# All merge gates computed ahead of the branch projections, 20 of 24 tiles by the Strassen scheme, and kept in DRAM

## The chip, the cores and the metric

The kernel runs on one core of one Trainium2 chip. The metric is the device time of one execution, in microseconds (us). The kernel before took 2695.42 us, the median of three runs (2694.82 to 2695.98).

The engines are named as in the profile: PE is TensorE (matmuls; its weight loads are PEld), DVE is VectorE, ACT is ScalarE, POOL is GpSimd and SP is SyncE, whose queue issues nearly all of the transfers. Each engine works through its own list of instructions in order.

## The reference, cut to what matters

One layer of a hybrid decoder block on 1024 tokens and 16 meta tokens, with a model width of 1024. Three branches (gated DeltaNet, Mamba-2 SSD, sliding-window attention) each give a 1024-wide output. Each is projected, weighted by a sigmoid gate per channel and token, and the three are added:

```python
u = rmsnorm(h, norm1_w[l]) @ w_in[l]
(..., gate_logits) = split_in(u)
gates = jax.nn.sigmoid(gate_logits)
g_a, g_b, g_c = jnp.split(gates, N_BRANCH, axis=-1)
merged = (g_a * (y_gdn @ w_proj_gdn[l]) + g_b * (y_ssd @ w_proj_ssd[l])
          + g_c * (y_swa @ w_proj_swa[l]))
h = h + merged @ w_out[l]
hn = rmsnorm(h, norm2_w[l])
h = h + jnp.square(jax.nn.relu(hn @ w_up[l])) @ w_down[l]
```

The gate logits are a product of the normed input (1024 x 1024 tokens) with 3 x 1024 columns of the input weights. The sigmoid is worked out as half of (1 + tanh of half the logit).

## The kernel before, in words

Activations lie transposed: 128 channels on the partitions, tokens along the row, in halves of 512 tokens. A matrix of 1024 channels is eight such tiles k by two halves c. Every fp32 operand is split into a high and a low part (ACT copies it to the rounded high part, DVE or POOL subtracts that from the original), and every product is three matmuls: high by high, high by low, low by high.

The normed input is kept all along as tiles hnh (high) and hnl (low). A gate tile is 128 of the 3 x 1024 gate channels of branch b, called (b, m) with m from 0 to 7: merge_gates loads and splits its weights (split_w: load to mgr, ACT copy mgh, POOL subtraction mgl) and runs for each half 24 matmuls into a bank mgm (gemm, L148); ACT's tanh (L1047) leaves the gate in a tile gt, of which there are four buffers. A projection tile (b, m) is merge_proj: weights wpr, split to wph and wpl, then 48 matmuls into two banks pr (L1063), and DVE operations that weight them with the gate and add them up in mg (L1070, L1073, L1074).

stage_merge walks the 24 tiles, all of branch 0 first. In each step it issues the gate tile two steps ahead and then the projection tile, so that PE goes from one to the other: 48 matmuls mgm, 48 matmuls pr, and so on. The first two gate tiles, and the weights of the third (w2), are issued during the attention branch. At the first tile of a branch, merge_load reads the branch's output back from DRAM: 16 halves, each loaded into one of four buffers yr (the ring "r"), copied to yh by ACT (L135) and subtracted to yl by DVE (L136). The 32 tiles yh and yl of one branch are one set of buffers, so that the next branch's take their place.

The order on each engine is set by a scheduler that places the instructions by its own estimate of when operands and buffers come free; the program's text is only its starting point. After the merge come stage_out (output projection, bank pso, L1115) and the MLP, whose up projection (bank up, L1209) is already done by the Strassen scheme, with the mixed activations prepared by u_mix.

Of the kernel before, what the change touches and what calls it, by code (L numbers as in the profile page):

```python
# [7 lines left out]
F32 = mybir.dt.float32  # L8
F32R = mybir.dt.float32r
U32 = mybir.dt.uint32  # L10
AF = mybir.ActivationFunctionType
ALU = mybir.AluOpType
# [4 lines left out]
P = 128  # L17
D = 1024
KT = D // P
SEQ = 1024  # L20
META = 16
# [27 lines left out]
W_M = 68  # L49
# [2 lines left out]
KW = SEQ + 4 * META  # L52
NM = 17
NPR = NFF // 2
HOIST = 2
WL, WR, WY, WS = 1800, 3200, 2000, 2200

# [5 lines left out]
class Trunk:  # L63
    def __init__(self, ctx, tc, I, out):
# [32 lines left out]
        self.gad = self.dram.tile([3 * KT, P, SEQ], F32, name="gad")  # L97
        self.acd = self.dram.tile([NPR, 7, P, 512], F32, name="acd")
        self.hd = self.dram.tile([NB, P, D], F32, name="hd")
# [939 lines left out]
    def gate_w(self, b, m):  # L1039
        return self.split_w(self.I["win"][W_M + KT * b + m], "mg")  # L1040

    def merge_gates(self, b, ms, w=None):
        nc = self.nc
        for m in ms:
            for c0, n, ps in self.gemm(w or self.gate_w(b, m), (self.hnh, self.hnl), CH_REAL, "mgm"):
                t = self.tp.tile([P, 512], F32, name="gt", tag="t", bufs=4)
                nc.scalar.activation(t, ps, AF.Tanh, scale=0.5)  # L1047
                self.gates[m, (c0 - META) // 512] = t

    def merge_load(self, b):  # L1050
        place = lambda n: self.half("y", 4 * KT, n)
        self.y = [[self.split_half(self.yd[b][k][:, 512 * c:512 * c + 512], "y", place, self.nc.vector)
                   for c in range(2)] for k in range(KT)]

    def merge_proj(self, b, m):
        nc = self.nc
# [19 lines left out]
    def stage_merge(self, w2):  # L1076
        self.mg = {}
        seq = [(b, m) for b in range(3) for m in range(KT)]
        for i, (b, m) in enumerate(seq):
            if m == 0:  # L1080
                self.merge_load(b)
            if i < len(seq) - 2:
                self.merge_gates(seq[i + 2][0], (seq[i + 2][1],), w2 if i == 0 else None)
            self.merge_proj(b, m)


    def stage_out(self):
# [63 lines left out]
    def split(self, src, hi, lo, eng=None):  # L1151
        nc = self.nc
        nc.scalar.activation(hi, src, AF.Copy)  # L1153
        (eng or nc.vector).tensor_tensor(lo, src, hi.bitcast(F32), op=ALU.subtract)  # L1154
        return hi, lo
# [154 lines left out]
    def stage_up(self):  # L1310
        self.u_prep(1)
        pre = [self.up_hoist(0)]
        for k in range(4):
            self.u_tile(1, k)
            self.u_tile(1, k + 4)
        pre += [self.up_hoist(j) for j in range(1, HOIST)]
        self.u_mix()
        for j in range(NPR):
            self.up_pair(j, pre[j] if j < HOIST else None)

    def stage_down(self):
# [12 lines left out]
        for p0, n in ((0, 6), (6, 5), (11, 5)):  # L1334
            first, lastc = p0 == 0, p0 + n == NPR
            prs = range(p0, p0 + n)
# [132 lines left out]
def build(ctx, tc, I, out):  # L1469
    k = Trunk(ctx, tc, I, out)  # L1470
    nc = tc.nc
    pool = lambda st, name, **kw: st.enter_context(tc.tile_pool(name=name, **{"bufs": 1, **kw}))
    ph, ps, px = ExitStack(), ExitStack(), ExitStack()
    k.px = ExitStack()
    k.pa = ExitStack()
    with nc.allow_non_contiguous_dma(reason="layout"):
        k.tp = pool(ctx, "tp")
        k.hn = pool(ph, "hn", side="right")
        k.c2 = pool(k.pa, "c2")
        k.sp = pool(ps, "smp", side="right")  # L1480
        k.xp = pool(px, "xp", side="right", bufs=3)
        k.stage_norm()
        px.close()
        k.open_branches()
        cur = k.gdn_first()
        k.stage_small()
        ps.close()
        k.open_gdn()
        k.stage_gdn(cur)
        k.open_rest()  # L1490
        k.stage_ssd()
        k.open_psum()
        store = k.stage_swa()
        k.gates = {}
        k.merge_gates(0, (0, 1))
        w2 = k.gate_w(0, 2)
        store()
        k.px.close()
        k.pa.close()
        k.pbx.close()  # L1500
        k.pdr = pool(ctx, "pdr", space=PSUM, reuse_waits="tile")
        k.lp = pool(ctx, "lp", reuse_waits="tile")
        k.stage_merge(w2)
        ph.close()
        k.rp = pool(ctx, "rp", side="right", reuse_waits="tile")
        k.stage_out()
        k.stage_mlp()
    return k
# [73 lines left out]
```

## Time and profile before

| what | value |
|---|---|
| median of three runs | 2695.42 us |
| the profiled execution | 2700.42 us |
| its span | 2698.7 us |
| PE busy | 2547.8 us (94%) |
| DVE, ACT, POOL busy | 1608.3, 1034.7, 614.7 us |
| stage that the change touches | 1419 to 1932 us of the span |
| HBM read, written | 179.56 MB, 52.70 MB |

A row of the chain of waits gives start, length and what it was: an engine's run of instructions, or a transfer that was waited for. The chain runs back from the end, so what stands in it set the end at that place. A row of the timeline gives start, length, engine, line, operation, the tiles written and read, sizes, how many, and in brackets the idle time of the engine before it and what ended it. A row of the windows gives busy time and count of each engine in a stretch, then the granted PE clock as a share, the DMA share and GB/s. Matmul ends are modelled, and a few records can be missing.

### The profile page before, as it was taken

How to read it: one execution, taken by the hardware profiler on the slowest of the kernel's cores; microseconds unless marked ns; L12 is line 12 of the kernel's file. 1: busy time of each engine (PE TensorE's matmuls, PEld its weight loads, DVE VectorE, ACT ScalarE, POOL GpSimd, SP SyncE). 2: the span in 40 equal slices, each digit the busy share in tenths (PEclk: the TensorE clock that was granted, in tenths of full speed). 3: DMA queues.
4: the chain of work that ended last, by engine and by line, in shares of the span. 5: the costliest groups of instructions: out<-in, count | busy, mean ns of one | idle time of the engine just before them, and what ended most of it. 6: DMA issues, size and time to landing. Idle time of an engine off the chain costs nothing.

```text
span 2698.7 us, 37432 instructions
## 1 busy us (share of the span) xinstructions
PE 2547.8 (94%) x13983; PEld 2178.5 (81%) x13983; DVE 1608.3 (60%) x3039; ACT 1034.7 (38%) x2581; POOL 614.7 (23%) x479
## 2 busy tenths in 40 slices
PE   6999999999999999999999999999998999989997
PEld 5887888887888988888887888878876888768886
DVE  5776767767466766577762022232428777586887
ACT  4434444434332332355552121121345444344443
POOL 3322222222133232321211222222340000040230
PEclk8989999999899999999999999999998999989999
DMA  3211211111111121321213131131323434655422
GB/s 117 70 37 53 61 53 53 53 36 60 47 55 63 63 79 63 95 56 52 60 48 125 47 110 47 47 109 48 129 100 127 164 149 152 241 191 192 143 92 86
DMA packets 120916, 241.14 MB, mean 89 GB/s; under 512 B 39478, under 2 KB 39894, under 8 KB 120734
## 3 DMA queue, kind: packets, MB, share of 16 engines
q1 hardware_dynamic: 116526, 230.98, 25.6%
q0 software_dynamic: 3200, 6.43, 1.2%
q8 instruction: 110, 1.80, 0.3%
q10 hardware_dynamic: 1008, 1.34, 0.2%
q14 instruction: 72, 0.59, 0.1%
HBM read 179.56 MB, written 52.70 MB: 86 GB/s over the span
## 4 chain that ended last, share of the span: by engine, by line
PE 75%; DVE 16%; issue 3%; DMA 2%; ACT 2%; POOL 1%; ACTq 0%; SPq 0%; DVEq 0%; POOLq 0%
PE dn L1365 11%; PE up L1209 11%; PE mgm L148 9%; PE pr L1063 9%; PE pso L1115 3%; PE aq L148 3%; PE x L148 3%; PE gg L148 2%; PE v L148 2%; PE q L148 2%; DVE xt L512 2%; PE z L148 2%; PE b L148 2%; PE c L148 2%; PE k L148 1%
## 5 line engine op out<-in xcount | busy, mean ns | idle before, releaser
L1154 POOL TENSOR_TENSOR wl<-wd,wh 128x512 fp32r<-128x512 f32 x48 | 71.6, 1497 | 521.7 <-DMA ar<-acd 340.1
L1365 PE MATMUL dn<-wh,ah 128*128 128x512 f32 x448 | 175.5, 393 | 14.5 <-ACT wh L1153 14.5
L1365 PE MATMUL dn<-wl,ah 128*128 128x512 f32 x448 | 176.2, 394 | 6.0 <-DVE wl L1154 5.4
L1365 PE MATMUL dn<-wh,al 128*128 128x512 f32 x448 | 175.6, 392 | 0.0
L1063 PE MATMUL pr<-yh,wph 128*128 128x512 f32 x384 | 150.0, 391 | 2.9 <-ACT yh L135 1.8
L1063 PE MATMUL pr<-yl,wph 128*128 128x512 f32 x384 | 150.1, 391 | 1.7 <-DVE yl L136 1.7
L1063 PE MATMUL pr<-yh,wpl 128*128 128x512 f32 x384 | 149.5, 389 | 0.0
L1073 DVE SCALAR_TENSOR_TENSOR gt<-gt,pr 128x512 f32<-128x512 f32 x32 | 21.9, 687 | 201.8 <-PE pr L1063 201.8
L1154 DVE TENSOR_TENSOR al<-ar,ah 128x512 fp32r<-128x512 f32 x112 | 98.7, 884 | 51.3 <-ACT ah L1153 51.1
L1153 ACT ACTIVATE ah<-ar 128x512 fp32r<-128x512 f32 x112 | 70.2, 627 | 125.0 <-PE dn L1365 90.5
L124 POOL TENSOR_TENSOR wpl<-wpr,wph 128x1024 fp32r<-128x1024 f32 x24 | 61.1, 2547 | 231.0 <-ACT wph L122 220.4
L1365 PEld LDWEIGHTS dn<-wh,ah 128*128 128x128 f32 x448 | 85.1, 190 | 32.9 <-ACT wh L1153 15.0
L122 ACT ACTIVATE wph<-wpr 128x1024 fp32r<-128x1024 f32 x24 | 25.5, 1061 | 215.0 <-PE pr L1063 195.6
L1365 PEld LDWEIGHTS dn<-wl,ah 128*128 128x128 f32 x448 | 85.1, 190 | 24.7 <-DVE wl L1154 6.1
L148 PE MATMUL mgm<-hnh,mgh 128*128 128x512 f32 x384 | 100.1, 398 | 2.1 <-ACT gt L1047 2.1
L148 PE MATMUL mgm<-hnl,mgh 128*128 128x512 f32 x384 | 99.9, 399 | 0.0
L148 PE MATMUL mgm<-hnh,mgl 128*128 128x512 f32 x384 | 99.5, 396 | 0.0
L1365 PEld LDWEIGHTS dn<-wh,al 128*128 128x128 f32 x448 | 85.2, 190 | 17.7
L124 POOL TENSOR_TENSOR mgl<-mgr,mgh 128x1024 fp32r<-128x1024 f32 x24 | 57.6, 2398 | 166.1 <-PE mgm L148 157.8
L1063 PEld LDWEIGHTS pr<-yh,wph 128*128 128x128 f32 x384 | 72.1, 188 | 20.2 <-ACT yh L135 3.7
L1063 PEld LDWEIGHTS pr<-yl,wph 128*128 128x128 f32 x384 | 72.1, 188 | 18.8 <-DVE yl L136 3.8
L148 PEld LDWEIGHTS mgm<-hnh,mgh 128*128 128x128 f32 x384 | 72.0, 189 | 18.8 <-ACT gt L1047 2.6
(477 smaller groups left out, 7080.4 us busy)
## 6 DMA issues: line engine op xcount, KB each, us to landing
ar<-acd SPq DMA_DIRECT2D x112, 256.0 KB
wu<-in_wup SPq DMA_DIRECT2D x34, 512.0 KB
acd<-s SPq DMA_DIRECT2D x64, 256.0 KB
mgr<-in_win SPq DMA_DIRECT2D x24, 512.0 KB
wpr<-in_wpr SPq DMA_DIRECT2D x24, 512.0 KB
yr<-yd SPq DMA_DIRECT2D x48, 256.0 KB
acd<-c SPq DMA_DIRECT2D x48, 256.0 KB
dms<-rowd SPq DMA_DIRECT2D x16, 512.0 KB
```

The source lines that it names most:

```text
L122: nc.scalar.activation(wh, wr, AF.Copy)
L124: nc.gpsimd.tensor_tensor(wl, wr, wh.bitcast(F32), op=ALU.subtract)
L148: nc.tensor.matmul(ps[:, 0:n], a[:, k, :], b[k][:, c0:c0 + n], start=(i == 0 and k == 0), stop=(i == 2 and k == KT - 1))
L512: nc.vector.tensor_tensor(tv, lb[:, j:j + 1, j + 1:32].broadcast_to([3 * n_, n, m]), ub[:, 0:n, j:j + 1].broadcast_to([3 * n_, n, m]), op= ...
L1063: nc.tensor.matmul(ps, x[:, k, :], y, start=(k == 0 and j == 0), stop=(k == KT - 1 and j == 2))
L1073: nc.vector.scalar_tensor_tensor(t, t, 1.0, ps, op0=ALU.add, op1=ALU.mult)
L1115: nc.tensor.matmul(ps, x[k, th][:, ts], y, start=(k == 0 and j == 0), stop=(k == KT - 1 and j == 2))
L1153: nc.scalar.activation(hi, src, AF.Copy)
L1154: (eng or nc.vector).tensor_tensor(lo, src, hi.bitcast(F32), op=ALU.subtract)
L1209: self.nc.tensor.matmul(ps, x[:, k * P:(k + 1) * P], ops[k][y], start=(j == 0 and k == 0), stop=(j == 2 and k == 3))
L1365: nc.tensor.matmul(acc[t], x[:, t * P:(t + 1) * P], y, start=(i == 0 and m == 0), stop=(i == n - 1 and m == 2))
```

## The change

All gates are computed before the first projection and go to DRAM. gate_out does the tanh and stores the half to a buffer gad in DRAM; gate_load reads a gate tile back into two of the four gt buffers, two tiles ahead of its use. Tiles 0 to 3 of branch 0 are computed as before. The other 20 form ten pairs of 256 gate channels. For these, the weights and the normed input are each taken as two by two blocks, and the four block products come from seven products of sums and differences (Strassen's scheme in Winograd's form): gp1 to gp7, each 12 matmuls (4 tiles k by 3 split products), together 84 instead of 2 x 48 = 96 for a pair.

gate_mix makes the mixed activations once: it adds hnh and hnl to get the normed input back (hr, in the four buffers of the ring "r"), forms the four sums and differences, and splits them to gh and gl, which lie in the 32 buffers that later take yh and yl. gate_pair makes the mixed and split weights (gah, gal, g1, g2, g3, g4, g22, mostly in the ring "m" of 17 halves), runs the seven products and adds them up to the four results (halves c11, u4, x1 and u2), which also live in ring "r".

After the pairs, the pool of the normed input is closed and a pool yp put in its place for the second branch's yh and yl, so that the outputs of the branches alternate between two sets; the next branch is read from the middle of the one before (m == 4), the first branch after the last pair.

```diff
--- before.py
+++ after.py
@@ -52,6 +52,7 @@
 KW = SEQ + 4 * META
 NM = 17
 NPR = NFF // 2
+NGP = 4
 HOIST = 2
 WL, WR, WY, WS = 1800, 3200, 2000, 2200
 
@@ -1039,18 +1040,136 @@
     def gate_w(self, b, m):
         return self.split_w(self.I["win"][W_M + KT * b + m], "mg")
 
+    def gate_out(self, g, c, ps):
+        t = self.tp.tile([P, 512], F32, name="gt", tag="t", bufs=4)
+        self.nc.scalar.activation(t, ps, AF.Tanh, scale=0.5)
+        self.nc.sync.dma_start(self.gad[g, :, 512 * c:512 * c + 512], t)
+
     def merge_gates(self, b, ms, w=None):
-        nc = self.nc
         for m in ms:
             for c0, n, ps in self.gemm(w or self.gate_w(b, m), (self.hnh, self.hnl), CH_REAL, "mgm"):
-                t = self.tp.tile([P, 512], F32, name="gt", tag="t", bufs=4)
-                nc.scalar.activation(t, ps, AF.Tanh, scale=0.5)
-                self.gates[m, (c0 - META) // 512] = t
+                self.gate_out(KT * b + m, (c0 - META) // 512, ps)
+
+    def gate_load(self, b, m):
+        for c in range(2):
+            t = self.gates[m, c] = self.tp.tile([P, 512], F32, name="gt", tag="t", bufs=4)
+            self.nc.sync.dma_start(t, self.gad[KT * b + m, :, 512 * c:512 * c + 512])
+
+    def gate_mix(self):
+        nc = self.nc
+        tt = nc.vector.tensor_tensor
+        g = self.go = {}
+        y = lambda n: self.half("y", 4 * KT, n)
+        sl = [slice(META + 512 * c, META + 512 * c + 512) for c in range(2)]
+        for k in range(4):
+            r = {}
+            for i in range(2):
+                for c in range(2):
+                    h, l = self.hnh[4 * i + k][:, sl[c]], self.hnl[4 * i + k][:, sl[c]]
+                    if (i, c) != (0, 1):
+                        g[{(0, 0): 0, (1, 0): 1, (1, 1): 2}[i, c], k] = h, l
+                    x = r[i, c] = self.half("r", 4, "hr", F32)
+                    tt(x, h.bitcast(F32), l.bitcast(F32), op=ALU.add)
+
+            def op(p, x):
+                h, l = g[p, k] = y("gh"), y("gl")
+                nc.scalar.activation(h, x, AF.Copy)
+                tt(l, x, h.bitcast(F32), op=ALU.subtract)
+            tt(r[0, 0], r[0, 1], r[0, 0], op=ALU.subtract)
+            op(4, r[0, 0])
+            tt(r[0, 0], r[1, 1], r[0, 0], op=ALU.subtract)
+            op(5, r[0, 0])
+            tt(r[0, 1], r[1, 1], r[0, 1], op=ALU.subtract)
+            op(6, r[0, 1])
+            tt(r[1, 0], r[1, 0], r[0, 0], op=ALU.subtract)
+            op(3, r[1, 0])
+
+    def gate_pair(self, g0, last):
+        nc = self.nc
+        tt = nc.vector.tensor_tensor
+        m = lambda n, dt=F32: self.half("m", NM, n, dt)
+        bank = (lambda n: self.pmm.tile([P, 512], F32, name=n, tag="mm", bufs=3))
+
+        def split(x, n):
+            h, l = m(n + "h", F32R), m(n + "l", F32R)
+            nc.scalar.activation(h, x, AF.Copy)
+            tt(l, x, h.bitcast(F32), op=ALU.subtract)
+            return h, l
+
+        def mm(ps, w, p):
+            for j, (x, y) in enumerate(((0, 0), (0, 1), (1, 0))):
+                for k in range(4):
+                    nc.tensor.matmul(ps, w[x][:, k * P:(k + 1) * P], self.go[p, k][y], start=(j == 0 and k == 0),
+                                     stop=(j == 2 and k == 3))
+        w1 = self.wst.tile([P, D], F32, name="gw1", tag="wr")
+        nc.sync.dma_start(w1, self.I["win"][W_M + g0])
+        w2 = self.wst.tile([P, D], F32, name="gw2", tag="wh")
+        nc.sync.dma_start(w2, self.I["win"][W_M + g0 + 1])
+        a = [w1[:, 0:512], w1[:, 512:D], w2[:, 0:512], w2[:, 512:D]]
+        ah = self.wst.tile([P, D], F32R, name="gah", tag="wl")
+        al = m("gal", F32R), m("gal", F32R)
+        nc.scalar.activation(ah, w1, AF.Copy)
+        for i in range(2):
+            tt(al[i], a[i], ah.bitcast(F32)[:, 512 * i:512 * i + 512], op=ALU.subtract)
+        ps = {}
+
+        def first():
+            ps[0] = self.pd("gp1")
+            mm(ps[0], (ah[:, 0:512], al[0]), 0)
+            x = self.half("r", 4, "x1", F32)
+            nc.scalar.copy(x, ps[0])
+            ps[1] = bank("gp2")
+            mm(ps[1], (ah[:, 512:D], al[1]), 1)
+            c = self.half("r", 4, "c11", F32)
+            tt(c, x, ps[1], op=ALU.add)
+            self.gate_out(g0, 0, c)
+            return x
+
+        def second():
+            s1 = m("gs1")
+            tt(s1, a[2], a[3], op=ALU.add)
+            o1 = split(s1, "g1")
+            tt(s1, s1, a[0], op=ALU.subtract)
+            o2 = split(s1, "g2")
+            s3 = m("gs3")
+            tt(s3, a[0], a[2], op=ALU.subtract)
+            tt(s1, a[1], s1, op=ALU.subtract)
+            ps[5] = self.pc("gp5")
+            mm(ps[5], o1, 4)
+            ps[6] = bank("gp6")
+            mm(ps[6], o2, 5)
+            return s1, s3
+        if last:
+            s4, s3 = second()
+            x1 = first()
+        else:
+            x1 = first()
+            s4, s3 = second()
+        u2 = self.half("r", 4, "u2", F32)
+        tt(u2, x1, ps[6], op=ALU.add)
+        o4 = split(s4, "g4")
+        p3 = self.pc("gp3")
+        o3 = split(s3, "g3")
+        p7 = bank("gp7")
+        for i in ((0, 1) if last else (1, 0)):
+            mm(*(((p7, o3, 6), (p3, o4, 2))[i]))
+        u4 = self.half("r", 4, "u4", F32)
+        tt(u4, u2, ps[5], op=ALU.add)
+        tt(u4, u4, p3, op=ALU.add)
+        self.gate_out(g0, 1, u4)
+        tt(u2, u2, p7, op=ALU.add)
+        o7 = split(a[3], "g22")
+        p4 = self.pc("gp4")
+        mm(p4, o7, 3)
+        tt(x1, u2, ps[5], op=ALU.add)
+        self.gate_out(g0 + 1, 1, x1)
+        tt(u2, u2, p4, op=ALU.add)
+        self.gate_out(g0 + 1, 0, u2)
 
     def merge_load(self, b):
-        place = lambda n: self.half("y", 4 * KT, n)
-        self.y = [[self.split_half(self.yd[b][k][:, 512 * c:512 * c + 512], "y", place, self.nc.vector)
-                   for c in range(2)] for k in range(KT)]
+        place = lambda n: self.half("y", 4 * KT, n, pool=self.yp if b == 1 else self.lp)
+        return [[self.split_half(self.yd[b][k][:, 512 * c:512 * c + 512], "y", place, self.nc.vector)
+                 for c in range(2)] for k in range(KT)]
 
     def merge_proj(self, b, m):
         nc = self.nc
@@ -1076,12 +1195,24 @@
     def stage_merge(self, w2):
         self.mg = {}
         seq = [(b, m) for b in range(3) for m in range(KT)]
+        self.gate_mix()
+        self.merge_gates(0, (2,), w2)
+        self.merge_gates(0, (3,))
+        for g0 in range(NGP, 3 * KT, 2):
+            self.gate_pair(g0, g0 == 3 * KT - 2)
+        y = self.merge_load(0)
+        self.ph.close()
+        self.yp = self.py.enter_context(self.tc.tile_pool(name="yp", bufs=1, side="right", reuse_waits="tile"))
+        for b, m in seq[0:2]:
+            self.gate_load(b, m)
         for i, (b, m) in enumerate(seq):
             if m == 0:
-                self.merge_load(b)
+                self.y = y
             if i < len(seq) - 2:
-                self.merge_gates(seq[i + 2][0], (seq[i + 2][1],), w2 if i == 0 else None)
+                self.gate_load(*seq[i + 2])
             self.merge_proj(b, m)
+            if m == KT // 2 and b < 2:
+                y = self.merge_load(b + 1)
 
 
     def stage_out(self):
@@ -1500,8 +1631,9 @@
         k.pbx.close()
         k.pdr = pool(ctx, "pdr", space=PSUM, reuse_waits="tile")
         k.lp = pool(ctx, "lp", reuse_waits="tile")
+        k.ph, k.py = ph, ExitStack()
         k.stage_merge(w2)
-        ph.close()
+        k.py.close()
         k.rp = pool(ctx, "rp", side="right", reuse_waits="tile")
         k.stage_out()
         k.stage_mlp()
```

How the engines' orders move. The names in the rows are tiles with a running number; an arrow goes from what is read to what is written.

ACT, from the last copy of the attention branch (yfa), before: the first copies are the weights of gate tile 3 (mgh) and the first branch's outputs (yh).

```order
L1017 COPY yfa_14156<-of_14503 128x128
L122 ACTIVATE mgh_14856<-mgr_14854 128x1024
L135 ACTIVATE yh_14646<-yr_14644 128x512
L135 ACTIVATE yh_14652<-yr_14650 128x512
L135 ACTIVATE yh_14658<-yr_14656 128x512
L135 ACTIVATE yh_14664<-yr_14662 128x512
```

ACT at the same place, now: the two tanhs of gate tile 2 (gt_14785 and gt_14813) stand ahead of the first copy of the mix.

```order
L1018 COPY yfa_14156<-of_14503 128x128
L1045 ACTIVATE gt_14785<-mgm_14760 128x512
L1045 ACTIVATE gt_14813<-mgm_14788 128x512
L1076 ACTIVATE gh_14657<-hr_14648 128x512
L1111 ACTIVATE gah_14882<-gw1_14878 128x1024
L1076 ACTIVATE gh_14662<-hr_14648 128x512
L1076 ACTIVATE gh_14667<-hr_14650 128x512
L1076 ACTIVATE gh_14672<-hr_14652 128x512
L1045 ACTIVATE gt_14847<-mgm_14822 128x512
L1076 ACTIVATE gh_14685<-hr_14676 128x512
```

The branch output copies have gone to the end of the gates; the copies of the mix (gh) wait behind the tanhs of tiles 2 and 3.

PE, now, in the first pair: gp1 and gp2 read the plain input, gp5 and gp6 the mixed one (gh, gl).

```order
L1102 MATMUL gp2_14903<-hnl_119,gah_14882 128x512 x4
L1102 MATMUL gp2_14903<-hnh_118,gal_14884 128x512 x4
L1102 MATMUL gp5_14935<-gh_14657,g1h_14923 128x512
L1102 MATMUL gp5_14935<-gh_14685,g1h_14923 128x512
L1102 MATMUL gp5_14935<-gh_14713,g1h_14923 128x512
L1102 MATMUL gp1_15039<-hnh_118,gah_15033 128x512 x4
L1102 MATMUL gp1_15039<-hnl_119,gah_15033 128x512 x4
L1102 MATMUL gp6_14948<-gh_14662,g2h_14928 128x512
L1102 MATMUL gp6_14948<-gh_14690,g2h_14928 128x512
L1102 MATMUL gp6_14948<-gh_14718,g2h_14928 128x512
L1102 MATMUL gp5_14935<-gh_14741,g1h_14923 128x512
L1102 MATMUL gp5_14935<-gl_14658,g1h_14923 128x512
```

Behind the third matmul of gp5 the order takes eight matmuls of the next pair (gp1_15039) and three of gp6 before it goes on with gh_14741, the fourth tile of the mix.

SP's queue, now, at the end of the gates: the stores of the last gates (to gad) and the loads of the first branch's outputs (yr).

```order
L1046 DMA gad_97<-gt_16317 128x512
L134 DMA yr_16388<-yd0_94 128x512
L134 DMA yr_16394<-yd0_94 128x512
L1046 DMA gad_97<-gt_16359 128x512
L1046 DMA gad_97<-gt_16381 128x512
L134 DMA yr_16400<-yd0_94 128x512
L1046 DMA gad_97<-gt_16385 128x512
L134 DMA yr_16406<-yd0_94 128x512
L134 DMA yr_16412<-yd0_94 128x512
L134 DMA yr_16418<-yd0_94 128x512
L134 DMA yr_16424<-yd0_94 128x512
L1056 DMA gt_16488<-gad_97 128x512
```

Before, the loads of the first branch stood at the beginning of the stage, with gate weights between them; now they stand among the last stores, and a gate load (gt_16488) comes after the seventh.

## The prediction

> **What bounds the kernel now.** I read the page's totals first, then the chain of waits, then busy time by window for the stage that the diff touches.
>
> ```profile
> span 2698.7 us, 37432 instructions
> PE 2547.8 (94%) x13983; PEld 2178.5 (81%) x13983; DVE 1608.3 (60%) x3039; ACT 1034.7 (38%) x2581; POOL 614.7 (23%) x479
> PE 75%; DVE 16%; issue 3%; DMA 2%; ACT 2%; POOL 1%; ACTq 0%; SPq 0%; DVEq 0%; POOLq 0%
> ```
>
> TensorE (PE) is busy for 94% of the span and is 75% of the chain that ended last. A matmul saved where PE is fed without a break is therefore worth its whole pace; elsewhere it is worth nothing. Which of the two the merge stage is, the chain tells:
>
> ```profile
> 1425.58 0.86 PE L148 MATMUL mgm<-hnh,mgh 128*128 128x512 f32 x3
> 1466.02 11.13 PE mgm L148 x48
> 1477.15 10.89 PE pr L1063 x48
> 1899.62 32.65 PE pr L1063 x144
> 1932.28 41.90 PE pso L1115 x183
> 1419.00:1932.00 513.00, 506.20 (x2190) 411.06 (x2189) 131.23 (x139) 108.75 (x153) 111.70 (x46) 1.00 0.25 82
> ```
>
> The first row is in the timeline, where tile 2's gate matmuls end at about 1425.7 and tile 3's begin; the next four are the chain; the last is the window of the whole stage (us; busy time and count of PE, weight loads, DVE, ACT, POOL; clock; DMA share; GB/s). I take 1419.0 as the stage's start, since the last attention matmuls end there, and 1932.3, where the output projection begins, as its end: 513.3 us. A gate tile is 48 matmuls in 11.13 us, 0.2319 each; a projection tile is 48 in 10.89 us, 0.2269 each. In the stage PE has 1036 gate matmuls left (22 tiles x 48, less 20 already done by 1419) and 24 x 48 = 1152 projection matmuls: 1036 x 0.2319 = 240.2, and 1152 x 0.2269 = 261.4, together 501.6. So only 11.7 us of the stage are lost, and these rows show where:
>
> ```profile
> 1429.89 4.58 DMA yr<-yd
> ...
> 1434.50 0.64 ACT yh L135
> 1435.16 0.71 DVE yl L136
> 1435.88 4.34 DMA yr<-yd
> 1441.69 3.66 DMA yr<-yd
> 1430.00:1440.00 10.00, 8.66 (x37) 6.20 (x35) 3.66 (x6) 3.60 (x6) 0.00 (x0) 1.00 0.79 267
> 1776.00:1790.00 14.00, 11.86 (x45) 9.19 (x44) 9.74 (x12) 7.76 (x12) 2.92 (x2) 0.88 0.63 205
> 1778.56 2.86 DVE L1074 TENSOR_TENSOR mg<-mg,gt 128x512 f32<-128x512 f32 x1
> 1782.11 2.83 PE L148 MATMUL mgm<-hnh,mgh 128*128 128x512 f32 x8 [2.14 <-ACT gt L1047]
> 1784.73 2.90 PE L148 MATMUL mgm<-hnl,mgh 128*128 128x512 f32 x8
> 1787.47 2.02 PE L148 MATMUL mgm<-hnh,mgl 128*128 128x512 f32 x8
> ```
>
> The 16 halves of a branch output pass through a ring of four buffers, and the chain goes from one landing to the next. By the waits in the chain the first branch costs some 7.6 us and the third some 4.0 us, of which about 1.7 us is slow matmuls: after 2.14 us of idle, two groups of eight took 2.83 and 2.90 us, and the third 2.02.
>
> **What the change saves.** Twenty gate tiles become ten pairs of 7 products x 12 matmuls, 84 for 96: 120 matmuls less. The nearest row for their pace is the MLP's up projection, which is the same scheme:
>
> ```profile
> 2064.47 291.96 PE up L1209 x1260
> 2064.00:2360.00 296.00, 294.74 (x1272) 240.56 (x1272) 208.85 (x291) 136.61 (x198) 0.00 (x0) 0.99 0.48 174
> ```
>
> 291.96 / 1260 = 0.2317 us. From 1419.0 there are now 76 plain gate matmuls (the 28 left of tile 2, and tile 3) and 840 of the pairs: 916 x 0.2317 = 212.2, a saving of 28.0. The projections stay at 261.4. Sum without losses: 473.6, or 39.7 under 513.3, because the old 11.7 go too. What comes in their place decides how much is kept.
>
> **New loss 1, the mix at the front.** Before the pairs can run, the normed input is rebuilt and mixed: 48 DVE operations and 16 ACT copies, with the first pairs' own splits between them.
>
> ```profile
> 1418.49 0.29 DVE L1011 TENSOR_TENSOR ot<-pv,rd 128x128 f32<-128x128 f32 x1 [1.84 <-PE pv L1007]
> 2051.82 7.31 DVE L1154 TENSOR_TENSOR ul<-u,uh 128x512 fp32r<-128x512 f32 x12
> 2035.62 0.69 DVE L1189 TENSOR_TENSOR u<-u 128x512 f32<-128x512 f32 x1 [0.81 <-ACT u L1180]
> 2036.42 0.69 DVE L1191 TENSOR_TENSOR u<-u 128x512 f32<-128x512 f32 x1
> 2050.80 6.35 ACT L1153 ACTIVATE uh<-u 128x512 fp32r<-128x512 f32 x12 [1.78 <-DVE u L1194]
> 1781.46 0.60 ACT L1047 ACTIVATE gt<-mgm 128x512 f32<-128x512 f32 x1 [2.68 <-DVE mg L1074]
> 2064.47 2.07 PE L1209 MATMUL up<-uh,sh 128*128 128x512 f32 x4 [5.65 <-ACT sh L1153]
> ```
>
> DVE is free at 1418.8 and does such operations every 0.609 us (7.31 / 12), or every 0.80 where each needs the one just before (2035.62 to 2036.42). In ACT's order, though, both tanhs of gate tile 2 stand ahead of the first copy of the mix, gh. The second of them waits for PE until 1425.7; then 0.60 of tanh and 0.63 of copy, and DVE goes on at 1427.1. From gl_14658 to the second writing of hr_14732 its order has 40 operations: 1427.1 + 40 x 0.609 = 1451.5; ACT's copy gh_14741 makes it 1452.4. PE reaches the matmul that reads gh_14741 after 114 matmuls (76 of plain gates, 24 of the first pair's first two products, 3 of gp5, 8 of the next pair's gp1 and 3 of gp6 that the order puts ahead of it), at 1419.0 + 114 x 0.2317 = 1445.4. That is 7.0 of waiting. A second stop, at gh_14746, costs 0.8: five DVE operations and a copy on, with nine matmuls between. The matmuls behind such a gap run slowly (the last row above: four in 2.07 after 5.65 of idle; by the rows of 1782, 1.7 us after a shorter one), for which I take 2.0. Loss 9.8. Bounds: if DVE never waits from 1418.8, the 46 operations to there end at 1446.8 and the loss is 2.3; at 0.80 each it is 14.6, with slow matmuls 16.6. I take 0.609, since in the up stage mixed and split operations kept that pitch wherever neighbours were independent, as most are here.
>
> The Trainium skill, VectorE: DVE Perf Modes, section The DRAIN you can't avoid, has it that a DVE operation does not start until the pipe of the one before is empty, and its errata section puts fp32 tensor_tensor at 691 ns. By that rule the 40 operations would take 27.6 and this loss would be 13.1; the row of twelve in 7.31 us does not agree with it.
>
> **New loss 2, the first branch's outputs.** They were hidden in part under gates before; now no gate matmul is left to cover them. The last buffer of the ring comes free only when the last gate (u2) has been added and gone through tanh, 2.0 us after PE's last gate matmul: 0.69 + 0.60 and hand-offs. Call that last matmul's end T. SP's queue has the gate stores between these loads, so loads 1 to 3 go at or before T, the fourth at T + 2.0. A buffer turns in 1435.88 - 1429.89 = 5.99 us. So the sixteenth half is issued at T + 2.0 + 3 x 6.0 = T + 20.0 and split 4.4 + 0.64 + 0.71 us later, at T + 25.8. PE's order weaves tiles 0 and 1 together, and 20 matmuls stand from the one that reads it: 4.5 us. The 96 of two tiles end at T + 30.3, instead of T + 21.8: 8.5 lost, and 2.0 for slow matmuls behind the gaps, 10.5. Bounds: at the 267 GB/s of the 1430 window a half takes 0.98 us, so the sixteenth is split at T + 2.0 + 12 x 0.98 + 5.8 = T + 19.6, and 2.3 is lost; if the last 20 run at the 0.36 us of 1782 to 1787 and 2.0 more follows, 13.
>
> The Trainium skill, TensorE: Matmul & The Clock Gate, section HAM oscillation, names PE gaps of more than about 3.4 us as those that cost the clock. The gaps in this loss are shorter than that, so by it the 2.0 here would fall away and the loss would be 8.5; the rows of 1782 disagree, with 0.88 of the clock after 2.14 us.
>
> **Parts that I cost at nothing.** (i) The ten pairs: each has 18 DVE operations, 11.0 us, and seven ACT splits or copies with four tanhs, under 7 us, beside 84 x 0.2317 = 19.5 us of PE. The up stage holds that pace with DVE at 208.85 of 296 us. If this cover goes, one hand-off a pair, 0.5, makes 5 in all. (ii) The 48 gate stores and 48 gate loads of 256 KB: on SP a load waits for DVE's last use of a gate buffer, with weight loads queued behind it; the three projection tiles in one run of x144 without a stop have a weight's landing (4.4 as for yr) and its split, 1.06 on ACT and 2.55 on POOL, within 10.9. (iii) Branches 2 and 3 are read from four tiles ahead, 4 x 10.89 us of PE work; the old 4.0 of the third goes. (iv) Everything behind 1932 keeps its order on every engine; x is loaded earlier, in branch 3. The rows behind (ii) are the page's:
>
> ```profile
> L122 ACT ACTIVATE wph<-wpr 128x1024 fp32r<-128x1024 f32 x24 | 25.5, 1061 | 215.0 <-PE pr L1063 195.6
> L124 POOL TENSOR_TENSOR wpl<-wpr,wph 128x1024 fp32r<-128x1024 f32 x24 | 61.1, 2547 | 231.0 <-ACT wph L122 220.4
> ```
>
> **The sum.** 473.6 + 9.8 + 10.5 = 493.9, against 513.3: 19.4 less. The profiled execution took 2700.42 us (1.7 beyond its span), and so 2681.0; the median of the three runs is 5.0 below the profiled one: 2676.
>
> **The rivals.**
> 1. Both losses at their lower bounds: 473.6 + 4.6 = 478.2, 35.1 less, 2660. For it: the 1430 window shows that the loads can go at 267 GB/s, and DVE was idle for 1.84 us before its last attention operation. Against it: DVE's order ties the mix to tile 2's tanh, and ring turns of 6 us are in the chain.
> 2. Both at their upper bounds, with 0.5 a pair: 473.6 + 16.6 + 13 + 5 = 508.2, 5.1 less, 2690. For it: the up stage's own mix takes PE down to 12.44 of 18 us, at 0.78 of the clock (the row below); beside POOL's weight split one DVE operation took 2.86 us (1778.56), against 0.609.
>
> ```profile
> 2036.00:2054.00 18.00, 12.44 (x52) 8.99 (x51) 17.69 (x29) 12.28 (x23) 0.00 (x0) 0.78 0.06 24
> ```
>
> 3. Slower: the pairs are not PE's but their operands'. In gate_pair g1, g2 and g4 come from one buffer, each by a DVE sum, an ACT copy and a DVE subtraction, 0.69 + 0.64 + 0.69 = 2.02. If the order does not prepare them a pair ahead, two such rounds show at gp6 and gp3: 4.0 a pair, 40 in all, 2716. The change turns into a loss from 1.9 a pair, one round. For it: the ring of four halves and the m ring of 17 are shared by neighbouring pairs (14 used by one). Against it: the up stage, with as dense a DVE, shows no such stop.
> 4. That nothing is saved would need PE to keep 96 matmuls a pair; its order lists 84, so I give this nothing of its own.
>
> **Chances.** Forecast 0.52, rival 1 0.20, rival 2 0.18, rival 3 0.10. A change of under 0.2%, 5.4 us, can't be told from none: faster is below 2690.0, slower above 2700.8. Half of rival 2 falls to the same: faster 0.81, same 0.09, slower 0.10. The range goes from 2660 to 2693; it leaves out rival 3 and the far sides of rivals 1 and 2.
>
> **What would show it.** PE idle of about 7 us ahead of gp5 on an ACT copy, at some 1445; pairs of 19.5 us; gaps under 3 us in the first two projection tiles, waiting for yr; from there x48 runs of 10.9 us. The forecast is wrong if PE waits inside the pairs for DVE or for a weight's high half, or if a gate load makes a projection's weights late.

## The result, and the profile after

| | median, us | before beside it | ratio, 95% interval |
|---|---|---|---|
| the change, first set | 2681.39 (4 runs) | 2695.70 | 0.9945 [0.9928, 0.9962] |
| the change, timed again | 2678.71 (5 runs) | 2697.35 | 0.9923 [0.9909, 0.9936] |

The change makes the kernel 14 to 19 us faster; 2676 was forecast, with a range from 2660 to 2693. Both intervals lie below 1, but the gain is under 1% and the times of one kernel lie up to 19 us apart (2663.36 to 2681.93 for mring below). In the twelve profiles of this study the last attention matmuls came between 1418.6 and 1427.4 us, while all that follows the stage took 766.2 to 767.3 in each. So the stage itself is compared in the traces, from the start of the last attention matmuls (bank of) to that of the output projection (pso).

The page of the changed kernel, and the end of its chain of waits:

```profile
span 2679.9 us, 37784 instructions
PE 2521.8 (94%) x13863; PEld 2154.7 (80%) x13863; DVE 1754.6 (65%) x3267; ACT 1072.8 (40%) x2647; POOL 565.5 (21%) x459
...
1664.93 248.13 PE pr L1182 x1082
1913.06 41.90 PE pso L1246 x183
```

There are 120 matmuls fewer, and from 1664.93 PE runs through the projections into the output projection without a stop. The rest of the span, from pso on, is 767.0 us, against 766.6 before: nothing moved there. All that PE waits for in the stage stands in the view of its waits (total us, times, longest), and the windows show where (the columns as in the prediction):

```profile
PE pr L1182 <- ACT yh L136: 4.5, 3, 2.0
PE gp L1102 <- ACT gh L1076: 4.4, 1, 4.4
PE gp L1102 <- ACT g2h L1095: 1.7, 1, 1.7
PE pr L1182 <- DVE yl L137: 0.2, 1, 0.2
```

```profile
1445.00:1455.00 10.00, 3.87 (x16) 2.56 (x15) 10.00 (x18) 3.06 (x6) 0.00 (x0) 0.82 0.00 0
1455.00:1465.00 10.00, 10.00 (x37) 8.06 (x38) 10.00 (x18) 5.99 (x10) 0.00 (x0) 0.84 0.27 83
1480.00:1640.00 160.00, 160.00 (x699) 130.97 (x698) 93.08 (x143) 56.13 (x88) 4.82 (x2) 1.00 0.31 107
1640.00:1650.00 10.00, 5.98 (x21) 3.42 (x20) 3.23 (x5) 4.11 (x8) 0.00 (x0) 0.97 0.69 213
1650.00:1660.00 10.00, 10.00 (x40) 8.11 (x39) 5.61 (x9) 5.03 (x9) 0.00 (x0) 0.86 0.83 272
```

One stop lies within the first pair, where its mixed products begin, and one at the first branch's outputs; in between the pairs keep PE busy for all of 160 us. In the first, DVE is busy without a break (10.00 of 10.00). The timeline gives the corners:

```profile
1421.73 0.27 PE L1016 MATMUL of<-ident,ot 128*128 128x128 f32 x1
1445.00 0.86 PE L1102 MATMUL gp<-gh,g1h 128*128 128x512 f32 x3
1449.45 0.96 PE L1102 MATMUL gp<-gh,g2h 128*128 128x512 f32 x3 [1.72 <-ACT g2h L1095]
1454.81 0.79 PE L1102 MATMUL gp<-gh,g1h 128*128 128x512 f32 x1 [4.40 <-ACT gh L1076]
1468.87 1.09 PE L1102 MATMUL gp<-hnh,gal 128*128 128x512 f32 x4
1640.47 0.39 PE L1182 MATMUL pr<-yh,wph 128*128 128x512 f32 x1
1429.67 0.69 DVE L1077 TENSOR_TENSOR gl<-hr,gh 128x512 fp32r<-128x512 f32 x1 [4.42 <-ACT gh L1076]
```

The stage runs from 1421.73 to 1912.90: 491.2 us. Its account:

- The first 100 matmuls, to 1445.00, take 23.3.
- From 1445.00 to 1468.87 are 68 matmuls of the first pairs in 23.9 us. At the pace of the rest, 171.6 us for the 748 matmuls from 1468.87 to 1640.47, 0.2294 each, they would take 15.6: **the front loses 8.3**, 6.1 of it idle.
- The projections take 1912.90 - 1640.47 = 272.4, or 11.0 over the 261.4 of before. Only part of that is the transition, as the second branch shows. Here are the same matmul in two neighbouring tiles of the second branch, and then of the third, each 48 matmuls apart:

```profile
1747.20 0.39 PE L1182 MATMUL pr<-yh,wpl 128*128 128x512 f32 x1
1758.40 0.39 PE L1182 MATMUL pr<-yh,wpl 128*128 128x512 f32 x1
...
1847.39 0.39 PE L1182 MATMUL pr<-yh,wpl 128*128 128x512 f32 x1
1858.27 0.39 PE L1182 MATMUL pr<-yh,wpl 128*128 128x512 f32 x1
```

11.20 us in the second branch, 10.88 in the third: 233.3 ns a matmul against 226.7, with no idle time in either. Over 384 matmuls **the second branch loses 2.5**, and **the transition 8.5**.

### The profile page after: what moved, and what is told of

It reads as the page before. It is cut to its first block, busy times and chain, and to the rows that moved or that the text cites. A ratio compares the mean times of both kernels' runs of the same rounds, so it can differ in the third digit from the quotient of the medians.

```text
span 2679.9 us, 37784 instructions
## 1 busy us (share of the span) xinstructions
PE 2521.8 (94%) x13863; PEld 2154.7 (80%) x13863; DVE 1754.6 (65%) x3267; ACT 1072.8 (40%) x2647; POOL 565.5 (21%) x459
## 5 line engine op out<-in xcount | busy, mean ns | idle before, releaser
L1182 PEld LDWEIGHTS pr<-yh,wpl 128*128 128x128 f32 x384 | 72.3, 188 | 16.0
L1340 PE MATMUL up<-uh,sh 128*128 128x512 f32 x256 | 71.8, 400 | 12.4 <-ACT sh L1284 6.5
L513 DVE TENSOR_TENSOR xt<-lb,ub 99x84 f32<-99x84 f32 (+23 forms) x248 | 78.2, 315 | 5.5
L1354 ACT ACTIVATE c<-c 128x512 f32<-128x512 f32 x64 | 40.3, 630 | 95.5 <-DVE c L1413 43.9
L1340 PE MATMUL up<-ul,sh 128*128 128x512 f32 x256 | 71.2, 400 | 0.0
```

The lines of the kernel that those rows point to most:

```text
L513: nc.vector.tensor_tensor(tv, lb[:, j:j + 1, j + 1:32].broadcast_to([3 * n_, n, m]), ub[:, 0:n, j:j + 1].broadcast_to([3 * n_, n, m]), op= ...
L1182: nc.tensor.matmul(ps, x[:, k, :], y, start=(k == 0 and j == 0), stop=(k == KT - 1 and j == 2))
L1340: self.nc.tensor.matmul(ps, x[:, k * P:(k + 1) * P], ops[k][y], start=(j == 0 and k == 0), stop=(j == 2 and k == 3))
L1354: self.nc.scalar.activation(dst, src, AF.Relu)
```

## The experiments

My theory: the gain is that of the 120 matmuls; what is lost again is a stop at the mix, a stop where the first branch passes through a ring of four, and a slower place of the second branch's operand in SBUF. The rival: the order itself brings the gain, or the stops only move when one is taken away. The stage lengths from the traces follow. Each is of one execution; the three of before lie within 5 us, the two of the change agree. The medians alone would not tell cover6, mring or dve0 from the change, since their intervals overlap with that of the change timed again; that of both does not.

| kernel | last attention matmuls | output projection | stage, us |
|---|---|---|---|
| before, first profile | 1419.0 | 1932.1 | 513.1 |
| before_again | 1419.9 | 1928.4 | 508.5 |
| before_third | 1422.7 | 1931.7 | 509.0 |
| plain | 1422.6 | 1926.5 | 503.9 |
| the change | 1421.7 | 1912.9 | 491.2 |
| after_again | 1421.4 | 1912.6 | 491.2 |
| cover6 | 1418.6 | 1904.9 | 486.3 |
| mring | 1423.1 | 1905.9 | 482.8 |
| dve0 | 1418.7 | 1899.9 | 481.2 |
| both | 1427.4 | 1904.6 | 477.2 |
| pad | 1422.7 | 1914.1 | 491.4 |
| swap | 1419.5 | 1914.1 | 494.6 |

### What the stage before really took

The kernel before, without an edit, profiled again, twice.

> The kernel before, unchanged, profiled once more. The changed kernel's profiled execution was 18.8 us under the first profile of before, but its median only 14.3 us under that of before. Theory A: the first profile of before was some 5 us long outside the merge stage; then this one shows the stage from the last attention matmuls to the output projection again at 513 us, and a span nearer 2694. Rival B: a profiled execution of this kernel is always longer; then the span is again about 2699.

> The kernel before once more, for the second stop of its stage (4.0 us at the third branch's outputs in the first profile, none in the second). Theory A (that stop comes from a rare long DVE operation and is chance): the stage takes 508 to 509 us again. Rival B (it is there in about every other execution): 512 to 513.

The second profile gave 2696.95 us with a stage of 508.5, the third 2700.36 with 509.0. The chain of the second, at the place where the first had its stop of 4.0 us:

```profile
1774.61 11.13 PE mgm L148 x48
1785.74 10.89 PE pr L1063 x48
```

There is no stop, in the third profile neither. Theory A of before_again was wrong on the place: the first profile was long inside the stage, by 4.6, not outside. Theory A of before_third has the length right: in these three, the stop at the third branch came once, with a DVE operation of 2.86 us. But long DVE operations are not rare. From 1420 to 1930 the first profile has 20 of over 1.5 us (the others 21 and 20), against 0.7 for most; each of the 20 begins while POOL subtracts a low weight part and ends 0.55 us after POOL does. What differs here is which operation met POOL's. First the first profile, then the second:

```profile
1778.33 2.54 POOL L124 TENSOR_TENSOR wpl<-wpr,wph 128x1024 fp32r<-128x1024 f32 x1 [12.30 <-ACT wph L122]
1778.56 2.86 DVE L1074 TENSOR_TENSOR mg<-mg,gt 128x512 f32<-128x512 f32 x1
...
1778.06 0.69 DVE L1074 TENSOR_TENSOR mg<-mg,gt 128x512 f32<-128x512 f32 x1
1778.44 2.58 POOL L124 TENSOR_TENSOR wpl<-wpr,wph 128x1024 fp32r<-128x1024 f32 x1 [12.19 <-ACT wph L122]
1779.26 2.31 DVE L136 TENSOR_TENSOR yl<-yr,yh 128x512 fp32r<-128x512 f32 x1
```

In the first, DVE came to this mg, which holds the gate buffer that the next tanh waits for, just after POOL had begun; in the second it came just before, and a yl was the long one. No run moved the two against each other on purpose, so that this is how the stop arose is read from the traces and not tried. The stage to compare with is about 508.7 us, and the change saves 17.5 us of it.

### The order without the pairs

```diff
-        self.gate_mix()
         self.merge_gates(0, (2,), w2)
-        self.merge_gates(0, (3,))
-        for g0 in range(NGP, 3 * KT, 2):
-            self.gate_pair(g0, g0 == 3 * KT - 2)
+        self.merge_gates(0, range(3, KT))
+        for b in (1, 2):
+            self.merge_gates(b, range(KT))
```

> The changed order with no Strassen pairs: all 24 gate tiles by the plain product, ahead of the projections and through DRAM, with no mix. Theory A (the whole gain is the 120 matmuls, the new order by itself gains and costs about nothing): 1036 gate matmuls x 0.2319 + 1152 x 0.2269 + about 11 lost where the first branch is read and in the second branch = 513, so about 2695, within 3 us of before. Rival B (the order itself brings part of the gain, because PE no longer changes between gates and projections): about 2686. Rival C (the round trip of the gates through DRAM costs): over 2700.

2691.92 us, ratio 0.9980 [0.9963, 0.9996]; the stage 503.9. In its chain the stage is two runs:

```profile
1422.90 240.01 PE mgm L149 x1036
1662.90 263.71 PE pr L1182 x1152
```

No theory had it right. Rival B was right that the order itself gains, but it is about 4.8 us of the stage, half of what it said, and not for its reason: 1036 gate matmuls take 240.01 us, 0.2317 each, as good as the 0.2319 of before. What is gained is that PE does not stop at the first branch at all. I had carried the transition's loss over from the changed kernel; but without the pairs the ring of four and the 32 buffers are free through all of the gates, and the loads of the halves are issued from 1424.86 to 1456.66, under them. 263.71 is 261.4 and the 2.3 to 2.5 of the second branch. So the order removes the old 7 us of the first branch and pays 2.4 for the place. The DRAM round trip of the gates costs nothing that the chain shows. The pairs bring 503.9 - 491.2 = 12.7: 120 matmuls, less the two stops.

### The stop at the front

```diff
-NGP = 4
+NGP = 6
-        self.merge_gates(0, (3,))
+        self.merge_gates(0, range(3, NGP))
```

> Six plain gate tiles instead of four ahead of the pairs, nine pairs: 96 matmuls more stand before the first one that reads the mix, 12 more in all. Theory A (the stop in front of the pairs, 6.1 us idle and 2.0 us of slow matmuls, is only a matter of cover): the stop is gone, 8.1 less and 2.8 more, about 5.3 us under the changed kernel, 2676. Rival B (DVE is behind through all of the first pairs, so the stop only moves): within 2 us of the changed kernel or slower by up to 2.8.

2672.89 us, ratio 0.9914 [0.9893, 0.9934]; the stage 486.3, 4.9 less than the change (5.3 expected). The windows at the place of the old stop, and over the pairs:

```profile
1445.00:1460.00 15.00, 15.00 (x67) 12.15 (x66) 14.83 (x26) 7.13 (x12) 0.00 (x0) 1.00 0.28 100
1480.00:1620.00 140.00, 140.00 (x612) 114.64 (x611) 81.15 (x124) 50.98 (x79) 2.40 (x1) 1.00 0.30 106
```

PE is busy throughout and the stop does not come back later, so it was cover that was missing: DVE catches up in two plain tiles. Twelve more matmuls, 2.8 us, pay for it.

### The ring of the first branch

```diff
-    def split_half(self, src, name, place, eng):
+    def split_half(self, src, name, place, eng, ring=("r", 4)):
         nc = self.nc
-        r = self.half("r", 4, name + "r", F32)
+        r = self.half(*ring, name + "r", F32)
...
-        return [[self.split_half(self.yd[b][k][:, 512 * c:512 * c + 512], "y", place, self.nc.vector)
+        return [[self.split_half(self.yd[b][k][:, 512 * c:512 * c + 512], "y", place, self.nc.vector, ("m", NM) if b == 0 else ("r", 4))
```

> The halves of the first branch's output are loaded into the ring of 17 that held the gate weights (free at the end of the gates) instead of the ring of four that the last gates still use. Theory A (the loss after the last gate matmul, 8.7 us of 11.2, is the ring of four: it turns every 5 to 6 us): the loads run ahead under the last pairs, the two first projection tiles take about 22 to 23 us instead of 29, and the time is 6 to 8 us under the changed kernel, about 2674. Rival B (the loads or the splits on ACT and DVE set the pace, not the ring): under 2 us gained.

2676.21 us, ratio 0.9915 [0.9892, 0.9939]; the stage 482.8, 8.4 less than the change. SP's queue issues eleven of the loads in one go, ahead of the last gate matmul, and the chain has no stop after the pairs (SP's timeline, then the chain):

```profile
1624.97 6.72 SPq L134 DMA_DIRECT2D yr<-yd  x11
1456.22 186.17 PE gp L1102 x802
1642.40 263.70 PE pr L1182 x1152
```

All of the transition's 8.5 was the ring. The 263.70 is that of the plain order, so the second branch's 2.4 is left, as it should be.

### Both together

Both diffs above.

> Six plain tiles ahead of the pairs and the ring of 17 for the first branch's halves, together. In the traces so far the stage from the last attention matmuls to the output projection took 491 us in the changed kernel, 486.3 with six plain tiles and 482.8 with the ring of 17. Theory A (the two stops are separate and add up): 491.2 - 4.9 - 8.4 = 477.9 us for the stage, PE without a stop in it, and a time about 13 us under the changed kernel, 2668. Rival B (one gain eats the other, because PE gets ahead of ACT and DVE as soon as both stops are gone): stage over 481.

2663.97 us, ratio 0.9871 [0.9849, 0.9894]; the stage 477.2, where 477.9 was expected. The chain of the whole stage:

```profile
1427.72 39.85 PE mgm L149 x172
1467.57 173.45 PE gp L1102 x756
1641.02 263.70 PE pr L1182 x1152
```

PE runs from end to end, at 0.2317, 0.2294 and 0.2289 us a matmul. The two stops were separate and their prices add up. This version beats both kernels, the one before by about 35 us (its ratio of 0.9871), the change by about 14 (by the ratios 0.9871 and 0.9923, each against the kernel before in its own set; by the stages 14.0).

### Who holds the start of the mix

On top of mring, the first tile's high parts by DVE:

```diff
-                nc.scalar.activation(h, x, AF.Copy)
+                if k:
+                    nc.scalar.activation(h, x, AF.Copy)
+                else:
+                    nc.vector.tensor_copy(h, x)
```

> On top of the ring of 17: the four high parts of the mix's first tile are copied by DVE instead of ACT, where they stood behind the tanhs of gate tile 2. Four more DVE operations (2.4 us), but DVE need not wait 4.4 us for ACT at the start. Theory A (the start of the mix is held by ACT's order): the stop ahead of the pairs falls from 6.1 us to about 4, the stage from 482.8 to about 480.5. Rival B (DVE's 46 operations alone set it, the wait for ACT is made up anyway): the stop grows by 2.4, the stage to about 485.

2671.48 us, ratio 0.9904 [0.9881, 0.9928]; the stage 481.2, 1.6 less than mring. PE's stops, and DVE at the start of the mix:

```profile
1445.15 0.49 PE L1105 MATMUL gp<-gh,g1h 128*128 128x512 f32 x1 [0.22 <-ACT gh L1077]
1448.16 0.49 PE L1105 MATMUL gp<-gh,g2h 128*128 128x512 f32 x1 [2.52 <-ACT gh L1077]
1448.77 2.00 PE L1105 MATMUL gp<-hnh,g4h 128*128 128x512 f32 x4
1450.56 1.89 PE L1105 MATMUL gp<-hnl,g4h 128*128 128x512 f32 x4
1453.27 0.50 PE L1105 MATMUL gp<-gh,g3h 128*128 128x512 f32 x1 [0.83 <-ACT g3h L1098]
1454.12 0.72 PE L1105 MATMUL gp<-hnh,g4l 128*128 128x512 f32 x2 [0.36 <-DVE g4l L1099]
1454.69 0.40 PE L1105 MATMUL gp<-gh,g1h 128*128 128x512 f32 x1
...
1427.08 0.69 DVE L1116 TENSOR_TENSOR gal<-gw,gah 128x512 fp32r<-128x512 f32 x1 [3.91 <-ACT gah L1114]
```

The idle time fell from 6.1 to 3.9, as theory A had it, but not for its reason: DVE still waits 3.91 us for ACT at the start, now for the first pair's weights (gah), which stand behind the same tanhs. Nor did the mix come sooner: DVE's first difference of the fourth tile begins at 1452.87, 34.2 us into the stage, against 31.8 in mring (1454.90). That is the 2.4 us that rival B reckoned with. By the trace, what shortened the idle time is PE's order, which moved with the edit: eight matmuls of the plain product gp3 (hnh and hnl with g4h) now stand ahead of the fourth tile's first matmul (1454.69), where in the change they come after it. In all 125 matmuls of the stage precede it, against 114. So this run says nothing on whether the order on ACT holds the start; that stays open.

### Place or alignment

Padding between the halves of the second branch:

```diff
...
+            i, self.ny = self.ny, self.ny + 1
+            if i:
+                self.yp.tile([P, 8], F32, name="pad", tag=f"pad{i}")
+            return self.yp.tile([P, 512], F32R, name=n, tag=f"y{i}")
```

> The changed kernel with 32 bytes between the 32 halves of the second branch's output, so that their addresses take every step of 32 bytes modulo 1024. In the changed kernel the second branch's projection matmuls come every 233.3 ns, those of the first and third every 226.7. Theory A (alignment: its halves start at 2016 modulo 2048, those of the others at 288): the pitch differs from half to half, and some come every 227 ns. Rival B (the place: these halves lie above 160 KB in a partition, the others between 58 and 125 KB): every half stays at 233 ns whatever its offset.

And the sets exchanged, with the first branch's loads issued once the normed input's pool is closed:

```diff
-        place = lambda n: self.half("y", 4 * KT, n, pool=self.yp if b == 1 else self.lp)
+        place = lambda n: self.half("y", 4 * KT, n, pool=self.lp if b == 1 else self.yp)
...
-        y = self.merge_load(0)
         self.ph.close()
         self.yp = self.py.enter_context(self.tc.tile_pool(name="yp", bufs=1, side="right", reuse_waits="tile"))
+        y = self.merge_load(0)
```

> The changed kernel with the two sets of halves exchanged: the first and third branch's outputs lie in the normed input's place (above 160 KB), the second's in the pool below 125 KB. Asked for the pitch of the projection matmuls alone; the first branch's halves can only be split once the last gate matmul has read the normed input, so the transition takes longer (8 to 15 us more). Theory A (the place sets it): the first and third branch's matmuls now come every 233 ns, the second's every 227. Rival B (something else of the second branch: its data, or what runs beside it): the second stays at 233, the others at 227.

In swap (2682.71 us in its one run) the two branches have changed roles. The same matmul, 48 apart, in the second branch and then in the third:

```profile
1746.93 0.39 PE L1182 MATMUL pr<-yh,wpl 128*128 128x512 f32 x1
1757.81 0.39 PE L1182 MATMUL pr<-yh,wpl 128*128 128x512 f32 x1
...
1847.35 0.39 PE L1182 MATMUL pr<-yl,wph 128*128 128x512 f32 x1
1858.55 0.39 PE L1182 MATMUL pr<-yl,wph 128*128 128x512 f32 x1
```

10.88 and 11.20: the slower pitch goes with the place, not with the branch. The 8 to 15 us more that were expected at the transition did not come: PE waits 4.0 us there for yh and yl, against 4.7 in the change. In pad (2682.62 us in its one run), by the distances between the starts of consecutive matmuls in its trace, the halves that the program puts between 162816 and 227296 bytes took means from 228.1 to 234.6 ns, each by its offset, 232.4 over all of them, and all those below 125216 bytes had a median of 227. So both theories hold a part: the offset shifts the pitch by some ns, but none of 32 offsets brings it to 226.7, and most of the loss goes with the place. What in the place does it stays open.

### The change once more

> The changed kernel, unchanged, timed in five more rounds, since single times of one kernel have differed by up to 10 us. Theory A (the gain is that of the stage: 508.5 or 513.3 to 491.2): 17 to 22 us under before, a ratio near 0.993, and a stage of 491 us again. Rival B (the first median, 14.3 us, is nearer): ratio 0.9945 or above.

2678.71 us against 2697.35, ratio 0.9923 [0.9909, 0.9936], and the stage again 491.2: theory A. The first set's 14.3 us was at the low end; its interval reaches to 19.4.

## Why the prediction was right, and where not

- **The matmuls saved.** 28.0 was forecast at 0.2317 a matmul; the mixed products came faster, 0.2294 over the pairs, and so 1.8 more was saved. Place fits this too: in PE's timeline of the change the twelve matmuls from 1460.62 to 1463.41 read hnh and hnl, in the upper place, at 0.2325 each, and the sixteen from 1464.33 to 1467.96 read gh and gl, in the lower, at 0.2269. The other pairs in (i) cost nothing, as forecast; rival 3 (operands late in each pair) is out, with 160 us of PE without a stop, and so the change sits on the faster side. Once, in the first pair, PE did wait for a weight's high half (1.72 us for g2h), which the prediction had named as a sign of being wrong.
- **Loss 1, the mix.** 9.8 forecast, 8.3 measured. DVE went on 7.9 us into the stage (1429.67 - 1421.73), where the working had 8.1, behind the tanh that the order showed. The stop at gh_14741 was 4.40 and not 7.0, since PE had already stood 1.72 at gp6 for the pair's own g2h, which the working left out.
- **Loss 2, the first branch.** 10.5 forecast, 8.5 measured, and mring shows that it was the ring of four. The last half's high part was ready at 1664.93, T + 24.5 with T at 1640.47; forecast for both parts T + 25.8. The two long gaps were about 2 us each, and matmuls behind them ran slowly: 0.86 of the clock in the window from 1650.

```profile
1644.20 0.73 PE L1182 MATMUL pr<-yh,wph 128*128 128x512 f32 x2 [1.98 <-ACT yh L136]
1648.17 0.73 PE L1182 MATMUL pr<-yh,wph 128*128 128x512 f32 x2 [2.04 <-ACT yh L136]
```

  The Trainium skill, TensorE: Matmul & The Clock Gate, section HAM oscillation, gives as its rule that PE must have no idle gaps of more than about 3.4 us. Here shorter ones cost the clock as well, so the rule does not cover this case.
- **The DVE pitch.** The mix ran at 0.60 us an operation. In DVE's timeline of the changed kernel, 17 operations start from the first of these rows up to the second:

```profile
1450.40 0.68 DVE L1077 TENSOR_TENSOR gl<-hr,gh 128x512 fp32r<-128x512 f32 x1
1460.63 0.68 DVE L1077 TENSOR_TENSOR gl<-hr,gh 128x512 fp32r<-128x512 f32 x1
```

  The 0.69 that followed from the section The DRAIN you can't avoid in the page VectorE: DVE Perf Modes of the Trainium skill is the length of one, not the distance between two. The same section adds that a next operation that is not held back starts earlier; the prediction left that out, and the trace agrees with it.
- **The step that failed: "The projections stay at 261.4".** The second branch's 384 matmuls take 2.5 us more because of the place of their operand. Nothing in the prediction looked at addresses, though the same trace had it: gate matmuls read that same place, at 0.2319, and projections the other, at 0.2269.
- **The second step that failed: "the old 4.0 of the third goes".** It was taken from one profiled execution, and two more profiles do not have it. The same stop was most of what made that execution 5.0 longer than the median, so that taking 5.0 off the profiled time and also counting 4.0 as gain used it twice. With a stage of 508.7 the forecast gain would have been 508.7 - 493.9 = 14.8, about 2681 from the same median; the measured stage gives 17.5, 2678, and the two sets 2681.4 and 2678.7.
- **Parts (ii) to (iv).** The gates' way through DRAM, the later branches' reads and everything after the stage cost nothing, as forecast.

The errors had both signs: 2.5 and 4.6 against the forecast, 1.8, 1.5 and 2.0 for it. So the mechanism of both losses was right, but that the time came out within 3 to 5 us of the forecast is in part luck: single terms were off by as much.

## What to carry to other kernels

Here the Strassen pairs saved their matmuls in full only when something plain ran while their operands were mixed, and when what comes next could already be read: two more plain tiles and a ring that is free at that moment gave 14 us on top of 17.5. When work that covered a load is moved away, look for the buffers that the load needs, not only for the transfer. And take a stop from one profile as a fact of the kernel only when a second profile has it too.

## What the runs showed that I had not expected

In these kernels the pitch of a matmul went with where its operand of 512 columns lies in SBUF. With the halves below 125 KB in a partition it was 226.7 ns, and above 160 KB 233.3 (swap: the same two numbers with the branches exchanged); offsets in steps of 32 bytes moved it between 228.1 and 234.6 there. The normed input, which the gates read, lies in that upper place as well.

A DVE operation on two tiles of SBUF that begins while POOL subtracts a low weight part is long, up to 2.90 us instead of 0.7, and ends 0.55 us after POOL does: so with all 20 long ones in the stage of the first profile. One that reads a bank of pr took 0.68 at such a place in the second profile.
